# Squares summed along rows by ScalarE, and the down projection's weights in the common buffers

## The chip, the cores and the metric

The kernel runs on one core of a Trainium2 chip. A core has TensorE (matrix products), VectorE, ScalarE and GpSimd (work on elements), SyncE (here it only issues transfers), a memory SBUF of 128 partitions, and accumulators in PSUM, the only place that TensorE writes to. The metric is the time of one execution on the device in microseconds (us), as the median of several.

## The reference

One decoder layer for 256 tokens of width 2048, all in float32. `h @ w` are the products; the sizes of the weights set the work.

```python
h = rmsnorm(x, norm_mix)
q, k, v, u = split(h @ w_in)                     # 2048 -> 4 x 1024
o_attn = differential causal attention(q, k, v)  # 4 heads, each normalized
o_pool = trailing means of u over 2/4/8/16 positions, minus u; then a product per group
x = x + concat(o_attn, o_pool) @ w_o             # 2048 -> 2048
hx, m = rmsnorm(x, norm_xattn), rmsnorm(mem, norm_mem)   # mem: 256 tokens of width 2048
x = x + cross attention of hx into m (wq, wkv, wo: 2048 -> 2048, 4096, 2048)
hf = rmsnorm(x, norm_ffn)
x = x + (silu(hf @ w_gate) * (hf @ w_up)) @ w_down       # 2048 -> 5632 -> 2048
return rmsnorm(x, norm_final)

def rmsnorm(x, g):   # mean over the features of each token
    return x * rsqrt(mean(x * x, axis=-1) + 1e-6) * g
```

## The kernel before

**Split operands.** TensorE is fed in a float32 form that rounds. So each operand is split: `split` (L126) lets ScalarE write the rounded part `hi` (L129, or L132 with a gain) and VectorE the rest, `lo = src - hi` (L130, L133). A product is then hi x hi + hi x lo + lo x hi: three matmuls (`mm3`, L217 to L219), or, where activations stand with hi and lo side by side in 512 columns, one of 512 and one of 256 columns (L163, L164).

**Weights.** `weights` (L139) brings 1 MB of a weight by SyncE's queue into one of three buffers `raw`, and splits it in two halves of 128x1024 into `whi` and `wlo`, also three buffers each. All products up to gate and up take their weights so. `gemm_tok` (L191, matmuls L209 to L211) makes values by tokens, `gemm_feat` (matmuls L163, L164) by features.

**Order.** A scheduler places the instructions on each engine; an engine works through its own in that order and waits where an input or a buffer isn't free. `between` holds generators, which `tick` advances once per half tile of weights: pieces of other work are written between the halves in this way.

**Norms.** The gain is multiplied in when activations are split; the factor 1/rms, one for each token, is applied after the product. It is needed with tokens on partitions (`col`) and along a row (`row`). Activations stand with features on partitions, so a token's squares are spread over 128 partitions and 16 tiles. For x (`norm_x`, L323) and the memory (`load_mem`, L515), `add_squares` (L267) lets ScalarE square 1024 columns (L270) and GpSimd add them up (L272, L275). After the output projection and the cross-attention, `residual` (L277) adds each finished tile to x, splits it, lets ScalarE square it (L286) and GpSimd add it to a total (L288). `rms` (L248) sums a total over partitions by four small matmuls against ones (L254). `along` transposes `col` into a row.

**Bands.** For the pooling, GpSimd makes eight banded matrices by selects (L355 to L359) and adds two pieces for each (L361).

**Down projection** (`prep`, L714, and the loop behind it). 44 feature tiles of the activations make 22 pairs; the output has two blocks `b` of 1024 columns. A pair with its 1 MB of weights is a product of 2x2 blocks: eight products, 24 matmuls of 512 columns, for a plain pair; seven, 21 matmuls, for the pairs in `FAST` (even numbers 0 to 12), which need sums of weight blocks (VectorE, L731 to L734) and of activations, and whose shared products are accumulated apart (`shared`) and added up at the end (`sums`). The pools `dn_r` (two raw buffers, one for sums), `dn_u` (four split buffers of 128x1024) and `dn_a` (two of 128x1536) are made when the pools of the gate's stage, `hid` and `wts` among them, are closed (`up.close()`, L699).

## Time and profile before

| what | value |
|---|---|
| median of 3 runs | 1438.62 us (1438.57 to 1440.9) |
| profiled execution, its time | 1442.4 us |
| profiled execution, its span | 1440.7 us |
| TensorE busy (matmul) | 1409.7 us, 98% |
| VectorE busy | 970.5 us, 67% |
| ScalarE busy | 731.7 us, 51% |
| GpSimd busy | 82.5 us, 6% |
| DMA engines' mean share | 52% |

The span is cut by the profile into stretches; in each one reads how long each engine was busy, the clock that TensorE was granted (1.00 is 2.4 GHz, 0.50 is 1.2 GHz), and what the DMA engines moved. A timeline gives each instruction with its start and, in brackets, how long its engine was idle before it and what ended that.

### The profile page before, as it was taken

The page shows a single profiled execution, that of the slowest core. Times are in us where ns is not written, and L with a number is a line of the kernel's source. Part 1 is how long each engine was busy: PE and PEld are TensorE (multiplying, and loading weights), DVE is VectorE, ACT ScalarE, POOL GpSimd, SP SyncE. Part 2 cuts the span into 40 slices and gives each one's busy share as a digit, 9 for nine tenths or more (in the row PEclk, how much of TensorE's full clock was granted, in tenths as well). Part 3 has the DMA queues.
Part 4 walks back from the last instruction along what each step waited for, and adds up shares of the span by engine and source line. Part 5 has one row for each costly group of instructions (what it writes and reads, how often), then busy time and mean ns, then how long its engine had stood idle before and what let it go on. Part 6 is the DMA issues. An engine that isn't in the chain of part 4 may idle for free.

```text
span 1440.7 us, 19291 instructions
## 1 busy us (share of the span) xinstructions
PE 1409.7 (98%) x7634; PEld 1213.7 (84%) x7634; DVE 970.5 (67%) x1298; ACT 731.7 (51%) x1058; POOL 82.5 (6%) x103
## 2 busy tenths in 40 slices
PE   7999999899999999999999999999999998999996
PEld 5888888788888888888888888888888886888885
DVE  7566868875556655567666666666666668858963
ACT  6455657554444444455554444544444445535543
POOL 6400002210000000011100000000000000000000
PEclk9999999999999999999999999999999999999998
DMA  6554536455554554465655555555555536556752
GB/s 247 193 182 164 182 131 234 163 198 180 180 201 147 175 176 151 150 210 197 203 200 181 199 180 201 179 202 179 201 178 202 178 145 231 206 196 202 249 205 112
DMA packets 42570, 269.72 MB, mean 187 GB/s; under 512 B 4848, under 2 KB 5872, under 8 KB 12784
## 3 DMA queue, kind: packets, MB, share of 16 engines
q1 hardware_dynamic: 40032, 262.16, 52.0%
q10 hardware_dynamic: 2448, 6.34, 1.3%
q8 instruction: 59, 0.97, 0.3%
q14 instruction: 31, 0.25, 0.0%
HBM read 264.29 MB, written 4.19 MB: 186 GB/s over the span
## 4 chain that ended last, share of the span: by engine, by line
PE 94%; DVE 3%; ACT 1%; DMA 1%; issue 1%; SPq 0%; ACTq 0%; DVEq 0%
PE acc L163 42%; PE acc L164 21%; PE acc L218 4%; PE acc L219 4%; PE acc L217 4%; PE acc L209 4%; PE acc L210 4%; PE acc L211 4%; PE ms L218 2%; PE ms L219 2%; PE ms L217 2%; DMA raw<-in_w_vu 1%; DVE hid L133 1%; DVE wlo L130 1%; DVE act L133 1%
## 5 line engine op out<-in xcount | busy, mean ns | idle before, releaser
L130 DVE TENSOR_TENSOR wlo<-raw,whi 128x1024 fp32r<-128x1024 f32 (+1 forms) x404 | 496.9, 1231 | 330.5 <-ACT whi L129 327.3
L163 PE MATMUL acc<-hid,whi 128*128 128x512 f32 x1920 | 669.5, 394 | 0.0
L129 ACT CAST whi<-raw 128x1024 fp32r<-128x1024 f32 (+1 forms) x404 | 420.4, 1041 | 459.0 <-PE acc L163 241.6
L164 PE MATMUL acc<-hid,wlo 128*128 128x256 f32 x1920 | 533.6, 278 | 0.0
L163 PEld LDWEIGHTS acc<-hid,whi 128*128 128x128 f32 x1920 | 360.1, 188 | 83.3
L164 PEld LDWEIGHTS acc<-hid,wlo 128*128 128x128 f32 x1920 | 361.0, 188 | 0.0
L163 PE MATMUL acc<-act,whi 128*128 128x512 f32 x768 | 274.0, 400 | 0.0
L164 PE MATMUL acc<-act,wlo 128*128 128x256 f32 x768 | 216.6, 282 | 4.0 <-DVE wlo L130 3.9
L163 PEld LDWEIGHTS acc<-act,whi 128*128 128x128 f32 x768 | 145.0, 189 | 34.6
L164 PEld LDWEIGHTS acc<-act,wlo 128*128 128x128 f32 x768 | 145.9, 190 | 5.0 <-DVE wlo L130 4.9
L130 DVE TENSOR_TENSOR ul<-raw,uh 128x1024 fp32r<-128x1024 f32 x60 | 72.7, 1222 | 39.4 <-ACT uh L129 39.3
L217 PE MATMUL acc<-uh,aC 128*128 128x512 f32 x240 | 93.4, 389 | 0.0
L218 PE MATMUL acc<-ul,aC 128*128 128x512 f32 x240 | 93.4, 389 | 0.0
L219 PE MATMUL acc<-uh,aC 128*128 128x512 f32 x240 | 93.4, 389 | 0.0
L129 ACT CAST uh<-raw 128x1024 fp32r<-128x1024 f32 x60 | 62.6, 1052 | 59.6 <-PE acc L219 54.0
L210 PE MATMUL acc<-wlo,hid 128*128 128x512 f32 x128 | 51.1, 399 | 6.9 <-DVE wlo L130 6.8
L288 POOL TENSOR_TENSOR row<-row,t 128x256 f32<-128x256 f32 x30 | 27.0, 899 | 460.4 <-ACT t L286 460.4
L217 PEld LDWEIGHTS acc<-uh,aC 128*128 128x128 f32 x240 | 45.1, 188 | 9.4
L219 PEld LDWEIGHTS acc<-uh,aC 128*128 128x128 f32 x240 | 45.1, 188 | 9.4
L218 PEld LDWEIGHTS acc<-ul,aC 128*128 128x128 f32 x240 | 45.1, 188 | 9.2
L209 PE MATMUL acc<-whi,hid 128*128 128x512 f32 x128 | 50.7, 400 | 0.9 <-ACT whi L129 0.9
L211 PE MATMUL acc<-whi,hid 128*128 128x512 f32 x128 | 50.6, 395 | 0.0
(201 smaller groups left out, 1454.5 us busy)
## 6 DMA issues: line engine op xcount, KB each, us to landing
raw<-in_w_gu SPq DMA_DIRECT2D x88, 1024.0 KB, 4.8
raw<-in_w_dn SPq DMA_DIRECT2D x44, 1024.0 KB, 4.8
raw<-in_w_qk SPq DMA_DIRECT2D x16, 1024.0 KB, 4.8
raw<-in_w_qx SPq DMA_DIRECT2D x16, 1024.0 KB, 4.8
raw<-in_w_kx SPq DMA_DIRECT2D x16, 1024.0 KB, 4.8
raw<-in_w_vx SPq DMA_DIRECT2D x16, 1024.0 KB, 4.8
raw<-in_w_vu SPq DMA_DIRECT2D x12, 1024.0 KB, 4.8
raw<-in_w_o SPq DMA_DIRECT2D x12, 1024.0 KB, 4.9
```

Of the source, the lines that this page charges most:

```text
L129: nc.scalar.copy(out=hi, in_=src)
L130: nc.vector.tensor_tensor(out=lo, in0=src, in1=hi.bitcast(F32), op=ALU.subtract)
L133: nc.vector.scalar_tensor_tensor(out=lo, in0=src, scalar=g, in1=hi.bitcast(F32), op0=ALU.mult, op1=ALU.subtract)
L163: nc.tensor.matmul(ps, whi[:, w], x, start=(k == 0), stop=False)
L164: nc.tensor.matmul(ps[:, :S], wlo[:, w], x[:, 0], start=False, stop=(k == nk - 1))
L209: nc.tensor.matmul(ps[t], xh, whi[:, w], start=(k == 0), stop=False)
L210: nc.tensor.matmul(ps[t], xh, wlo[:, w], start=False, stop=False)
L211: nc.tensor.matmul(ps[t], xl, whi[:, w], start=False, stop=(k == KT - 1))
L217: nc.tensor.matmul(ps, l[0], r[0], start=start, stop=False)
L218: nc.tensor.matmul(ps, l[0], r[1], start=False, stop=False)
L219: nc.tensor.matmul(ps, l[1], r[0], start=False, stop=stop)
L288: nc.gpsimd.tensor_tensor(out=tot, in0=tot, in1=sq, op=ALU.add)
```

## The change

It has three parts, and a few constants that follow from them (`PAD` keeps the places of pools in memory).

**Squares by rows.** `add_squares` and `norm_x` go, and `rms` stays for one norm alone. `row_squares` loads x, or the memory, once more with tokens on partitions (new inputs `x_rows`, `mem_rows`; two transfers of 1 MB each on SyncE's queue), and ScalarE squares 1024 columns at a time and sums them along the row in the same instruction (`accum_out`). VectorE adds the two halves. For the norm before gate and up, the row copies of x that `to_rows` makes anyway are squared in this way, and the factor is made after the first two tiles of gate and up instead of after the first. `residual` keeps its squares for the cross-attention's norm only, and VectorE adds them instead of GpSimd. The band matrices' additions also go to VectorE.

**Weights of the down projection.** The pool `wts` is now opened first and lives to the end. `prep` takes `raw`, `whi` and `wlo` from it (three buffers each); sums of weight blocks are written over raw blocks or into a small buffer `sum`. A pair with seven products hands out its parts in four pieces of two, two, two and one block instead of three of three, two and two.

**Which pairs.** `FAST` becomes the nine even numbers 2 to 18; pairs 0 and 1 are plain.

```diff
-FAST = tuple(range(0, 14, 2))
+FAST = tuple(range(2, 20, 2))
...
+    wts = ctx.enter_context(tc.tile_pool(name="wts", bufs=3, side="right"))
     hid = up.enter_context(tc.tile_pool(name="hid", bufs=4, side="right"))
-    wts = up.enter_context(tc.tile_pool(name="wts", bufs=3, side="right"))
...
+    def row_squares(src, r):
+        ss = const.tile([P, 2, 2], F32, name=name("ss"))
+        for t in range(2):
+            raw = slot(F32)
+            nc.sync.dma_start(out=raw, in_=src[:, t])
+            for _ in range(2):
+                yield
+            for h in range(2):
+                part = raw[:, h * 1024:(h + 1) * 1024]
+                nc.scalar.activation(out=part, in_=part, func=AF.Square, accum_out=ss[:, t, h:h + 1])
+                yield
+        rc = const.tile([P, 2], F32, name=name("rc"))
+        nc.vector.tensor_reduce(out=rc, in_=ss, axis=AX.X, op=ALU.add)
+        r["col"] = rsqrt(rc, rc, D)
+        yield
+        r["row"] = t_row()
+        nc.vector.tensor_copy(out=r["row"], in_=along(rc))
...
-        sq = tot if f == 0 else t1()
-        nc.scalar.activation(out=sq, in_=x, func=AF.Square)
-        if 0 < f and (into is not None or f < KT - 1):
-            nc.gpsimd.tensor_tensor(out=tot, in0=tot, in1=sq, op=ALU.add)
+        if tot is not None:
+            sq = tot if f == 0 else t1()
+            nc.scalar.activation(out=sq, in_=x, func=AF.Square)
+            if f:
+                nc.vector.tensor_tensor(out=tot, in0=tot, in1=sq, op=ALU.add)
...
-    between.append(norm_x())
+    between.append(row_squares(a["x_rows"], r_x))
...
-            nc.gpsimd.tensor_tensor(out=band[:, kt, g], in0=b, in1=dgn, op=ALU.add)
+            nc.vector.tensor_tensor(out=band[:, kt, g], in0=b, in1=dgn, op=ALU.add)
...
-            add_squares(tot, c, raw)
...
+        yield from row_squares(a["mem_rows"], r_m)
...
+            nc.scalar.activation(out=t2(), in_=tp, func=AF.Square, accum_out=ss_x[:, t, q:q + 1])
...
-    nc.vector.tensor_copy(out=rb_f, in_=along(rms(tot2)))
     ps_u = gemm_feat(hf, a["w_gu"][1])
     finish()
+    rc_f = const.tile([P, 2], F32, name="rc_f")
+    nc.vector.tensor_reduce(out=rc_f, in_=ss_x, axis=AX.X, op=ALU.add)
+    rb_f = const.tile([P, S], F32, name="rb_f")
+    nc.vector.tensor_copy(out=rb_f, in_=along(rsqrt(rc_f, rc_f, D)))
...
-        raw = dn_r.tile([P, 4, 512], F32, tag="raw", name=name("raw"))
+        raw = wts.tile([P, 4, 512], F32, tag="raw", name=name("raw"))
...
-        s = dn_r.tile([P, 4, 512], F32, tag="sum", bufs=1, name=name("sum"))
-        nc.vector.tensor_tensor(out=s[:, 0:2], in0=b12[:, None].to_broadcast([P, 2, 512]), in1=raw[:, 0:2], op=ALU.subtract)
-        yield halves(raw[:, 0:3], 3, dn_a, "a")
-        nc.vector.tensor_tensor(out=s[:, 2], in0=b22, in1=s[:, 0], op=ALU.subtract)
-        nc.vector.tensor_tensor(out=s[:, 3], in0=b21, in1=s[:, 2], op=ALU.subtract)
-        yield halves(s[:, 0:2], 2, dn_u, "u")
-        yield halves(s[:, 2:4], 2, dn_u, "u")
+        yield parts(raw[:, 0:2])
+        s = dec.tile([P, 2, 512], F32, tag="sum", bufs=2, name=name("sum"))
+        less(s, b12[:, None].to_broadcast([P, 2, 512]), raw[:, 0:2])
+        yield parts(s)
+        less(b12, b22, s[:, 0])
+        yield parts(raw[:, 2:4])
+        less(b22, b21, b12)
+        yield parts(raw[:, 1:2], 1)
...
-            if p == 14 and FAST:
+            if p in FAST[-1:]:
                 between.append(sums(b, [shared[0], None, shared[1], shared[2], shared[3]]))
```

How the instructions stand then is shown at three places. GpSimd's queue at the start, before (`act` is the total of squares and then the bands, `t` the selects):

```order
L357 AFFINE_SELECT t_65_518<-t_65_518 128x256
L272 TENSOR_TENSOR act_322<-act_322 128x1024 x3
L275 TENSOR_TENSOR act_322<-act_322 128x512
L275 TENSOR_TENSOR act_322<-act_322 128x256
L361 TENSOR_TENSOR act_493<-t_60_499,t_61_500 128x256
L361 TENSOR_TENSOR act_493<-t_62_506,t_63_507 128x256
L359 AFFINE_SELECT t_66_519<-t_64_513 128x256
```

and the same queue, now:

```order
L353 AFFINE_SELECT t_65_512<-t_65_512 128x256
L355 AFFINE_SELECT t_66_513<-t_64_507 128x256
L350 MEMSET t_67_519 128x256
L355 AFFINE_SELECT t_68_520<-t_64_507 128x256
L351 AFFINE_SELECT t_67_519<-t_67_519 128x256
L344 MEMSET t_69_526 128x256
L353 AFFINE_SELECT t_67_519<-t_67_519 128x256
```

Five additions of squares and the bands' additions are gone from it; the selects follow each other, as buffers come free.

VectorE's queue at the entry of the down projection, before (`raw` to `ul` are the first pair's weights, `t1f` and `aC` the last activations):

```order
L661 TENSOR_TENSOR t1f_10712<-acc_10669,t1f_10712 128x256
L691 TENSOR_TENSOR t1f_10712<-t1f_10712,rb_f 128x256
L661 TENSOR_TENSOR t1f_10760<-acc_10717,t1f_10760 128x256
L694 TENSOR_TENSOR t1f_10760<-t1f_10760,rb_f 128x256
L696 TENSOR_TENSOR t1f_10668<-t1f_10712,t1f_10760 128x256
L130 TENSOR_TENSOR aC_10568<-t1f_10668,aC_10568 128x256
L731 TENSOR_TENSOR sum_10793<-raw_10791 128x1024
L733 TENSOR_TENSOR sum_10793<-raw_10791,sum_10793 128x512
L734 TENSOR_TENSOR sum_10793<-raw_10791,sum_10793 128x512
L130 TENSOR_TENSOR al_10796<-raw_10791,ah_10795 128x1536
L130 TENSOR_TENSOR ul_10811<-sum_10793,uh_10810 128x1024
```

and now (the first row is the first half of pair 0):

```order
L130 TENSOR_TENSOR wlo_10739<-raw_10736,whi_10738 128x1024
L653 TENSOR_TENSOR t1f_10667<-acc_10624,t1f_10667 128x256
L683 TENSOR_TENSOR t1f_10667<-t1f_10667,rb_f 128x256
L130 TENSOR_TENSOR wlo_10755<-raw_10736,whi_10754 128x1024
L716 TENSOR_TENSOR sum_10816<-raw_10804 128x1024
L130 TENSOR_TENSOR wlo_10773<-raw_10770,whi_10772 128x1024
L653 TENSOR_TENSOR t1f_10715<-acc_10672,t1f_10715 128x256
L716 TENSOR_TENSOR raw_10804<-raw_10804,sum_10816 128x512
L686 TENSOR_TENSOR t1f_10715<-t1f_10715,rb_f 128x256
L688 TENSOR_TENSOR t1f_10623<-t1f_10667,t1f_10715 128x256
L130 TENSOR_TENSOR aC_10523<-t1f_10623,aC_10523 128x256
L130 TENSOR_TENSOR wlo_10789<-raw_10770,whi_10788 128x1024
```

The first pair's splits have moved from behind the last activations to ahead of them, between the evictions of the last tiles of gate and up.

VectorE's queue a little further on in the down projection, at the second pair with seven products, before:

```order
L130 TENSOR_TENSOR ul_10821<-sum_10793,uh_10820 128x1024
L130 TENSOR_TENSOR ul_10833<-raw_10830,uh_10832 128x1024
L130 TENSOR_TENSOR ul_10849<-raw_10830,uh_10848 128x1024
L731 TENSOR_TENSOR sum_10866<-raw_10864 128x1024
L733 TENSOR_TENSOR sum_10866<-raw_10864,sum_10866 128x512
L130 TENSOR_TENSOR al_10869<-raw_10864,ah_10868 128x1536
L734 TENSOR_TENSOR sum_10866<-raw_10864,sum_10866 128x512
L130 TENSOR_TENSOR ul_10884<-sum_10866,uh_10883 128x1024
L130 TENSOR_TENSOR ul_10894<-sum_10866,uh_10893 128x1024
```

and now, at the first such pair (pair 2; `sum_10893` belongs to pair 4):

```order
L130 TENSOR_TENSOR wlo_10807<-raw_10804,whi_10806 128x1024
L716 TENSOR_TENSOR raw_10804<-raw_10804 128x512
L130 TENSOR_TENSOR wlo_10819<-sum_10816,whi_10818 128x1024
L716 TENSOR_TENSOR sum_10893<-raw_10881 128x1024
L130 TENSOR_TENSOR wlo_10830<-raw_10804,whi_10829 128x1024
L130 TENSOR_TENSOR wlo_10841<-raw_10804,whi_10840 128x512
L130 TENSOR_TENSOR wlo_10850<-raw_10847,whi_10849 128x1024
L716 TENSOR_TENSOR raw_10881<-raw_10881,sum_10893 128x512
L130 TENSOR_TENSOR wlo_10866<-raw_10847,whi_10865 128x1024
L130 TENSOR_TENSOR wlo_10884<-raw_10881,whi_10883 128x1024
L716 TENSOR_TENSOR raw_10881<-raw_10881 128x512
```

Before, a pair's first sum stood with its own pair's splits. Now it stands ahead of the last two splits of the seven-product pair before it; in later pairs it stands behind those and ahead of the plain pair's.

## Rows read from the trace of the kernel before

**Rows 1.** Page's span and TensorE's share (busy us, share, instructions)

```profile
span 1440.7 us, 19291 instructions
...
PE 1409.7 (98%) x7634; PEld 1213.7 (84%) x7634; DVE 970.5 (67%) x1298; ACT 731.7 (51%) x1058; POOL 82.5 (6%) x103
```

**Rows 2.** Waits of TensorE: us in total, times, longest us

```profile
PE acc L210 <- DVE wlo L130: 6.8, 5, 3.9
PE ms L217 <- ACT ah L129: 4.5, 1, 4.5
PE acc L164 <- DVE wlo L130: 3.9, 2, 2.6
```

**Rows 3.** Three stretches: length, busy us by engine, granted clock, DMA share, GB/s

```profile
14.00:36.00 22.00, 15.41 (x57) 11.32 (x56) 19.87 (x17) 12.34 (x19) 16.39 (x12) 0.92 0.68 256
...
240.00:269.00 29.00, 25.03 (x131) 20.95 (x130) 28.82 (x34) 17.63 (x29) 15.02 (x10) 0.94 0.48 171
1189.00:1200.50 11.50, 6.59 (x22) 4.65 (x21) 9.14 (x11) 6.04 (x7) 0.00 (x0) 0.70 0.64 222
```

**Rows 4.** Timeline of TensorE at the start: start us, us, operation, [idle before]

```profile
17.15 0.39 PE L209 MATMUL acc<-whi,hid 128*128 128x512 f32 x1
18.87 0.50 PE L210 MATMUL acc<-wlo,hid 128*128 128x512 f32 x1 [1.33 <-DVE wlo L130]
...
27.55 0.39 PE L209 MATMUL acc<-whi,hid 128*128 128x512 f32 x1
31.81 0.52 PE L210 MATMUL acc<-wlo,hid 128*128 128x512 f32 x1 [3.87 <-DVE wlo L130]
...
34.26 0.63 PE L210 MATMUL acc<-wlo,hid 128*128 128x512 f32 x1
34.69 0.63 PE L211 MATMUL acc<-whi,hid 128*128 128x512 f32 x1
```

**Rows 5.** Same time on VectorE, GpSimd and ScalarE

```profile
14.46 0.69 DVE L130 TENSOR_TENSOR wlo<-raw,whi 128x512 fp32r<-128x512 f32 x1
...
16.35 2.47 DVE L130 TENSOR_TENSOR wlo<-raw,whi 128x512 fp32r<-128x512 f32 x1 [0.80 <-ACT whi L129]
...
15.88 2.39 POOL L272 TENSOR_TENSOR act<-act 128x1024 f32<-128x1024 f32 x1 [8.94 <-ACT act L270]
...
16.91 1.71 ACT L132 ACTIVATE hid<-x_sb,sm 128x256 fp32r<-128x256 f32 x4 [0.60 <-DMA x_sb<-in_xT]
18.52 1.03 ACT L129 CAST whi<-raw 128x1024 fp32r<-128x1024 f32 x1
```

**Rows 6.** Output projection: VectorE and GpSimd

```profile
236.62 0.48 DVE L133 SCALAR_TENSOR_TENSOR act<-act,sm,act 128x256 fp32r<-128x256 f32 x1
...
241.50 2.62 DVE L133 SCALAR_TENSOR_TENSOR hid<-x_sb,sm,hid 128x256 fp32r<-128x256 f32 x1
...
240.99 2.85 POOL L272 TENSOR_TENSOR act<-act 128x1024 f32<-128x1024 f32 x1 [1.16 <-ACT act L270]
```

**Rows 7.** Stretches: the DMA queue backed up; down projection's first block

```profile
20.00:22.00 2.00, 1.16 (x6) 0.65 (x5) 2.00 (x4) 2.00 (x4) 1.40 (x1) 1.00 1.08 416
...
1200.50:1311.00 110.50, 110.50 (x489) 91.55 (x488) 84.19 (x80) 54.70 (x51) 0.00 (x0) 1.00 0.59 205
```

**Rows 8.** VectorE while GpSimd makes selects

```profile
48.23 1.75 DVE L130 TENSOR_TENSOR wlo<-raw,whi 128x1024 fp32r<-128x1024 f32 x1 [1.28 <-ACT whi L129]
```

**Rows 9.** Chain of waits: start us, us, piece (a norm's sums; the pace)

```profile
706.20 0.34 PE ms L254 x4
...
1202.69 0.23 PE acc L218
```

**Rows 10.** Groups by line: count, busy us, mean ns, idle before

```profile
L130 DVE TENSOR_TENSOR ul<-raw,uh 128x1024 fp32r<-128x1024 f32 x60 | 72.7, 1222 | 39.4 <-ACT uh L129 39.3
...
L734 DVE TENSOR_TENSOR sum<-raw,sum 128x512 f32<-128x512 f32 x14 | 9.6, 684 | 0.0
```

**Rows 11.** Page's DMA issues: count, KB, us to landing

```profile
raw<-in_w_dn SPq DMA_DIRECT2D x44, 1024.0 KB, 4.8
```

78 lines of the change are left out of this document (25 added, 53 removed).

## The prediction

> **What bounds the kernel now.** I read the page first: TensorE is busy for 1409.7 us of a span of 1440.7 us [rows 1]. A matmul's end is modelled, so that share says only that every microsecond won must be one in which TensorE stands still or runs slowly, or a matmul left out. Next I read whom TensorE waits for [rows 2]. All that counts is three waits on a split of a weight (ScalarE casts the high part, VectorE subtracts for the low one): 6.8 us and 3.9 us for VectorE's low parts, 4.5 us for ScalarE's cast. Third, I cut the span into stretches [rows 3]: these waits lie in 14 to 36 us (the first projection), 240 to 269 us (the output projection, while the memory's activations are split beside it) and 1189 to 1200.5 us (the entry of the down projection). There the granted clock falls below 1.00 and TensorE is idle; elsewhere it keeps its pace.
>
> What a stretch loses is its idle time, what slow matmuls cost, and some 0.27 us at each stop, since the last matmul's busy time reaches 0.16 us past its turn and the first after a stop takes 0.11 us longer. The start: 22.00 - 15.41 = 6.6 us idle [rows 3], in four stops, of which the first and last stand in [rows 4]. After the last, nine matmuls come 0.43 us apart [rows 4] instead of 0.23, at the level of 1.2 GHz after an idle 3.87 us: 9 x 0.20 = 1.8 us. With 4 x 0.27 that is 9.5 us. The output projection: 29.00 - 25.03 = 4.0 us idle; a clock of 0.94 over 29 us means about 3.5 us at half speed, so 1.7 us lost; three stops give 0.6: 6.2 us, an estimate. The entry: 11.50 - 6.59 = 4.9 us idle, nine slow matmuls 1.8 us, two stops 0.6: 7.3 us.
>
> **Why VectorE is late there.** At the start a subtraction of 128x512 takes 2.47 us where the seven of its size before it take 0.62 to 0.80 (the last of them 0.69) [rows 5]; GpSimd's addition of squares began just ahead, at 15.88 us, and ran 2.39 us. At 241.5 us it is the same: 2.62 us for a split that took 0.48 us at 236.6, under a GpSimd addition of 2.85 us [rows 6]. Two engines off the chain, summing squares for norms, stop the chain.
>
> The Trainium skill (SBUF — State Buffer, Who interferes with whom) says that a VectorE instruction with two SBUF inputs contends with a GpSimd instruction that reads SBUF, and the later one blocks until the other is done. The rows agree: 16.35 + 2.47 ends 0.55 us after GpSimd's 18.27.
>
> **The change part by part.**
>
> *Squares of x.* The four squares on ScalarE and GpSimd's five additions leave the start; with them goes the cause of the stops. What is late next is the DMA queue: the cast of the third weight tile cannot start before 18.52 us [rows 5], since ScalarE first has four splits of x that landed at 16.9. Then the cast 1.03, VectorE 1.2: TensorE goes on at about 20.8 us, not at 21.6, and stood still for about 2.0 us from 18.5 (17.15 [rows 4] and six matmuls). The rest of that projection then has its splits in time, VectorE needing about 4.1 us per tile (2 x 1.22 and four splits of x at 0.4) against 24 x 0.227 = 5.5 us of TensorE. So 9.5 - 2.0 - 0.2 = **7.3 us** are won.
>
> Instead x is loaded a second time by rows, 2 x 1 MB on SP's queue, one ahead of the second, one ahead of the fourth weight tile of the next projection. The weights queue behind them. The DMA engines moved 416 GB/s while backed up [rows 7], so 1 MB is 2.5 us; each tile is wanted 5.5 us after the one before and has over 3 us in hand: nothing. The squares (four, each like a cast of its size, 1.03 us [rows 5], and a read of the sum) and the reduction lie beside the second projection's matmuls; then the root, and v's evictions, which release the accumulators that the third projection needs. In the order they stand ahead of the last tile's splits, 5 us before TensorE wants them: nothing. But the eight additions for the bands go from GpSimd to VectorE, between v's evictions and the second tile's split of the third projection. Eight x 0.42 us on VectorE (estimated below), with GpSimd's selects making their inputs. While such selects ran, VectorE's split took up to 1.75 us instead of 1.22 [rows 8]. By my count of that queue the split is done about when it is wanted. Bounds: 0, and 1.5 us (three instructions lengthened by 0.5 us); I take **0.4 us lost**, near the lower end because the splits after it have slack again. By the skill's rule taken strictly, each of the eight additions could stand behind a whole select; the sum would then be 8 x 0.4 = 3.2 us of VectorE, and the loss about 2 us rather than 0.4.
>
> *Squares of the memory, and of the sums after the output projection.* The memory's squares move to the next projection (4 on ScalarE, 2 x 1 MB on SP), where a tile of weights takes TensorE 5.6 us and ScalarE about 3: hidden. In 240 to 269 us, VectorE loses the long waits (three of about 2.1 us, and shorter ones under GpSimd's smaller additions) and takes GpSimd's additions of 256 columns, one per feature tile of 5.6 us, about 0.42 us each (an estimate: 512 columns take 0.69 [rows 10]). It was busy for all of this stretch before; without about 8 us of waiting and with 2 us of additions it is at some 75%. So the stops go: **6.0 us won**; if the additions ahead of a split still cost one stop, 3.
>
> *Three norms without a sum over partitions.* `rms` on TensorE goes for x, the memory and the feed-forward norm; each is 0.34 us [rows 9]: **1.0 us**. The third norm's transposes move behind the first gate and up tiles. Their chain (square, reduce, load of the root's table, root, reciprocal) ends some 8 us after the last x tile, and eleven matmuls stand ahead of the transposes; ScalarE has 1 us or more free per cast there: nothing. Its squares, now eight of 512 columns in the row copies for sixteen of 256, stand ahead of the stores to DRAM, which nobody waits for until the down projection.
>
> *Entry of the down projection.* Before, its buffers were new pools over memory of the gate's tiles, and its first pair needed a sum and splits of three parts; now raw and splits come from the same pool as all weights, and the first pair is plain. Transfer, cast and subtraction of pair 0 stand ahead of the last evictions, and TensorE goes from the last up tile straight into pair 0. What is late next is the last up tile's eviction (behind a 1.05 us cast, then 0.37 and 0.42 us), which frees the fourth accumulator; it is wanted after twelve matmuls, 2.7 us. All 7.3 us of the entry go, or 0.2 of them stay: **7.2 us won**.
>
> *Nine pairs with seven products.* Two more pairs of 22, in two blocks, each with three matmuls fewer: 12 x 0.23 us [rows 9] = **2.7 us**, if VectorE keeps up. For two pairs it has six instructions of 1.22 us and three of 0.69 [rows 10]: 9.4 us at most, against (24 + 21) x 0.227 = 10.2 us of TensorE. It fits; VectorE was at 76% before [rows 7].
>
> *Three buffers instead of up to six.* A tile's cast waits until TensorE has left the tile three before. Cast 1.05, subtraction 1.22, and 0.2 for the signals: 2.5 us; for the first tile of a plain pair TensorE has in that time only the last two tiles of the seven, 6 + 3 matmuls, 2.05 us, and one or two on the high part. So TensorE may wait 0 to 0.3 us at each of 18 places; I take 0.05, since the high part's matmuls go ahead: **0.9 us lost**, bounds 0 and 5.4. And in the second block VectorE's queue has the sum for pair 4, which waits for its transfer of 4.8 us [rows 11], ahead of a split of pair 2; the evictions of the first block make this the tightest place. 0 to 2 us; **0.5 us lost**.
>
> The sum: 7.3 + 6.0 + 1.0 + 7.2 + 2.7 = 24.2, less 0.4 + 0.9 + 0.5 = 1.8: **22.4 us won**. The profiled execution took 1442.4 us, of which 1.7 lie around the span; it would become 1420.0. The median of the other runs lies 3.8 us lower, at 1438.6, and the same gain gives **1416.2 us**.
>
> **The rivals.** (1) *Three buffers are too few*: the handover costs its upper bound, 5.4 us, and the second block's start 2: 1422 us. For it: the margin is a few tenths. Against it: the gate's tiles, on the same three buffers, wait nowhere. (2) *The start and the output projection keep part of their stops*, because the loads by rows delay weights (2 x 2.5 us at most) or VectorE, now with the additions, is still late (3 us): 1421 us. Against it: slack of 3 us and a load of 75%. (3) *Slower than before*: VectorE's queue stands at each sum of the next seven-product pair until its weights land, and all splits queue behind. There are 18 such sums; it decides from 1.25 us at each, since 18 x 1.25 = 22.5 us eats the gain; at 2 us, 1452 us. For it: the buffer is freed by the last split of the pair three before, and VectorE has then only about 5 us of work ahead of the sum, little more than the 4.8 us of the transfer. Against it: VectorE is held back by TensorE's pace, which adds some 2 us. (4) *It does not do what it says*: pair 0's weights cannot be split early, since the memory or the queue holds them, and the entry stays: 1423 us.
>
> **How the numbers follow.** The forecast 0.72 (1411 to 1420: upper gains, no new waits, and up to 3 us for the pace of matmuls with moved buffers), (1) 0.10, (2) 0.09, (4) 0.03, (3) 0.05, nothing measurable 0.01. A range from 1411 to 1424 leaves out (3) and parts of the tails. Faster by over 0.2% (2.9 us, about what a measurement of this kernel can tell from no change): 0.94; within: 0.01; slower: 0.05.
>
> **What would show it.** No wait of TensorE on a split over 1 us after 25 us; granted clock 1.00 in 26 to 36, 232 to 262 and around the entry; VectorE's splits at the start at 0.5 and 1.2 us throughout; the third projection's first tiles and the pairs of the down projection without stops. Wrong if TensorE waits in each pair, or if VectorE's sums wait for weights.

## The result and the profile after

The changed kernel took 1425.09 us (median of 4 executions, 1421.82 to 1426.48), the kernel before in the same comparison 1439.76 us (4, 1438.57 to 1441.32): a ratio of 0.9894 with a 95% interval of 0.9873 to 0.9916. That is 14.7 us won; 22.4 had been forecast, with a range that ended at 1424. A second comparison (the first experiment below) gave 1423.05 us against 1440.61, a ratio of 0.9877 (0.9858 to 0.9896), 17.6 us. So the sign and most of the mechanism were right, and 5 to 8 us of the gain are missing.

The page of the changed kernel, which answers to [rows 1]:

```profile
span 1422.6 us, 19276 instructions
...
PE 1404.4 (99%) x7610; PEld 1208.7 (85%) x7610; DVE 967.5 (68%) x1361; ACT 742.3 (52%) x1083; POOL 23.6 (2%) x55
```

TensorE has 24 instructions fewer, GpSimd is down from 82.5 to 23.6 us. Whom TensorE waited for (us in total, times, longest), all that is left of its waits on a split [rows 2]:

```profile
PE acc L210 <- DVE wlo L130: 1.5, 3, 0.8
PE acc L209 <- ACT whi L129: 1.5, 2, 1.1
```

The waits of 3.9, 2.6 and 4.5 us are gone. The same stretches as in [rows 3], moved by what was won ahead of them, and at the end the stretch of the down projection that answers to the second of [rows 7] (length, busy us of TensorE, its weight loads, VectorE, ScalarE, GpSimd, then the granted clock, DMA share, GB/s):

```profile
14.00:36.00 22.00, 20.35 (x88) 15.89 (x87) 13.63 (x20) 14.54 (x22) 0.00 (x0) 1.00 1.01 411
232.00:262.00 30.00, 30.00 (x174) 26.26 (x173) 27.00 (x49) 19.70 (x34) 0.00 (x0) 1.00 0.67 240
1173.00:1184.50 11.50, 11.50 (x59) 9.59 (x58) 8.98 (x13) 5.49 (x9) 0.00 (x0) 1.00 0.74 268
1184.50:1295.00 110.50, 110.43 (x481) 89.19 (x480) 92.65 (x98) 60.31 (x66) 0.00 (x0) 1.00 0.59 201
```

The granted clock is 1.00 in all of them, and of the first three TensorE stands still only in that at the start, for 1.65 us instead of 6.59. But look at the last: in 110.5 us there were 489 matmuls before [rows 7], and there are 481 now, with hardly any idle time shown. At the pace of [rows 9] eight matmuls are 1.8 us.

To see where the time went, the start of the same matmul is looked up in both traces, at the seams of the stages. "Again" is the second profiled execution of the changed kernel.

| stage, from one seam to the next | before, us | after | again | won | won again | forecast |
|---|---|---|---|---|---|---|
| start to the third projection's first matmul | 61.45 | 53.99 | 53.89 | 7.5 | 7.6 | 7.6 |
| third projection (to 83.31, 77.14, 77.05) | 21.86 | 23.15 | 23.16 | -1.3 | -1.3 | -0.4 |
| from there to gate and up's last matmul | 1106.72 | 1100.24 | 1099.54 | 6.5 | 7.2 | 6.7 |
| from that to the down projection's last | 237.13 | 231.34 | 231.08 | 5.8 | 6.1 | 8.5 |
| to the end of the span | 13.54 | 13.88 | 13.82 | -0.3 | -0.3 | 0 |
| span | 1440.7 | 1422.6 | 1421.5 | 18.1 | 19.2 | 22.4 |

(Of the three norms at 0.3 us, the first is in the forecast's first row, the two others are in the third.) Two stages fall short: the third projection by 0.9 us, the down projection by 2.4 to 2.7.

**The third projection.** TensorE, then VectorE, then GpSimd:

```profile
66.35 0.50 PE L210 MATMUL acc<-wlo,hid 128*128 128x512 f32 x1 [0.79 <-DVE wlo L130]
```

```profile
63.49 0.60 DVE L357 TENSOR_TENSOR act<-t,t 128x256 fp32r<-128x256 f32 x1 [1.26 <-POOL t L353]
64.74 0.43 DVE L357 TENSOR_TENSOR act<-t,t 128x256 fp32r<-128x256 f32 x1 [0.64 <-POOL t L353]
65.08 3.49 DVE L130 TENSOR_TENSOR wlo<-raw,whi 128x1024 fp32r<-128x1024 f32 x3
```

```profile
63.78 0.57 POOL L355 TENSOR_SCALAR_AFFINE_SELECT t<-t 128x256 f32<-128x256 f32 x1
64.31 0.40 POOL L353 TENSOR_SCALAR_AFFINE_SELECT t<-t 128x256 f32<-128x256 f32 x1
```

VectorE isn't busy ahead of the late subtraction: it stands still for 1.26 and 0.64 us, since the band additions (L357) stand in its queue and wait for GpSimd's selects. The eight additions themselves take 0.41 to 0.60 us, near the 0.42 of the estimate.

**The down projection.** The view of waits names what ScalarE's casts wait for there, a buffer that TensorE still reads, and in the second line what holds up TensorE's weight loads (PEld), 20 times.

```profile
ACT whi L129 <- PE ms L219: 14.6, 24, 0.7
...
PEld acc L218 <- DVE wlo L130: 6.4, 20, 0.6
```

One of the 20 places, on ScalarE, VectorE and TensorE:

```profile
1201.88 1.06 ACT L129 CAST whi<-raw 128x1024 fp32r<-128x1024 f32 x1 [0.69 <-PE ms L219]
```

```profile
1201.99 1.22 DVE L716 TENSOR_TENSOR sum<-raw 128x1024 f32<-128x1024 f32 x1
1203.12 1.22 DVE L130 TENSOR_TENSOR wlo<-raw,whi 128x1024 fp32r<-128x1024 f32 x1
```

```profile
1203.72 0.84 PE L217 MATMUL acc<-whi,aC 128*128 128x512 f32 x3
1204.40 0.50 PE L218 MATMUL acc<-wlo,aC 128*128 128x512 f32 x1
1204.74 0.40 PE L219 MATMUL acc<-whi,aC 128*128 128x512 f32 x1
```

This is the first tile of a plain pair. Three matmuls on the high part have run ahead; the fourth needs the low part, which VectorE ends at 1204.34. The matmul starts at 1204.40 and the next 0.34 us later instead of 0.23: the 0.11 us after a stop that the prediction had read from [rows 4], here after a stop too short to show as idle time. Over the 1001 intervals of the down projection the excess over 0.2267 us is 4.3 us (again: 4.0), some 0.2 us for each of the 20 places on the mean, from 0.1 us where only the restart is paid to 0.6. Two causes offer themselves in these rows: the buffer (the cast stood 0.69 us waiting for it), and the sum (1.22 us) in VectorE's queue ahead of the subtraction, whose cast had ended at 1202.94.

### The profile page after: what moved, and what is told of

The parts are those of the page before. It is cut to its first block, busy times and chain, and to the rows that moved or that the text cites. A ratio compares the mean times of both kernels' runs of the same rounds, so it can differ in the third digit from the quotient of the medians.

```text
span 1422.6 us, 19276 instructions
## 1 busy us (share of the span) xinstructions
PE 1404.4 (99%) x7610; PEld 1208.7 (85%) x7610; DVE 967.5 (68%) x1361; ACT 742.3 (52%) x1083; POOL 23.6 (2%) x55
## 4 chain that ended last, share of the span: by engine, by line
PE 93%; DVE 2%; DMA 2%; ACT 1%; POOL 1%; issue 0%; SPq 0%; DVEq 0%
PE acc L163 44%; PE acc L164 22%; PE acc L218 4%; PE acc L219 4%; PE acc L210 4%; PE acc L211 4%; PE acc L209 3%; PE acc L217 3%; PE ms L218 2%; PE ms L219 2%; PE ms L217 2%; DVE wlo L130 1%; DMA raw<-in_w_dn 1%; DMA raw<-in_w_vu 1%; ACT whi L129 0%
## 5 line engine op out<-in xcount | busy, mean ns | idle before, releaser
L130 DVE TENSOR_TENSOR wlo<-raw,whi 128x1024 fp32r<-128x1024 f32 (+1 forms) x510 | 606.5, 1196 | 360.7 <-ACT whi L129 357.6
L129 ACT CAST whi<-raw 128x1024 fp32r<-128x1024 f32 (+1 forms) x510 | 523.2, 1029 | 527.0 <-PE acc L163 250.6
L163 PE MATMUL acc<-hid,whi 128*128 128x512 f32 x1920 | 670.7, 393 | 0.0
L164 PE MATMUL acc<-hid,wlo 128*128 128x256 f32 x1920 | 538.1, 280 | 0.0
L163 PEld LDWEIGHTS acc<-hid,whi 128*128 128x128 f32 x1920 | 359.6, 187 | 80.8
L164 PEld LDWEIGHTS acc<-hid,wlo 128*128 128x128 f32 x1920 | 362.9, 189 | 0.0
L163 PE MATMUL acc<-act,whi 128*128 128x512 f32 x768 | 271.9, 398 | 0.0
L164 PE MATMUL acc<-act,wlo 128*128 128x256 f32 x768 | 215.5, 281 | 0.0
L163 PEld LDWEIGHTS acc<-act,whi 128*128 128x128 f32 x768 | 144.2, 188 | 34.0
L164 PEld LDWEIGHTS acc<-act,wlo 128*128 128x128 f32 x768 | 145.1, 189 | 0.2
L218 PE MATMUL acc<-wlo,aC 128*128 128x512 f32 x208 | 83.1, 399 | 0.4
L219 PE MATMUL acc<-whi,aC 128*128 128x512 f32 x208 | 81.2, 390 | 0.0
L217 PE MATMUL acc<-whi,aC 128*128 128x512 f32 x208 | 75.2, 390 | 0.0
L218 PEld LDWEIGHTS acc<-wlo,aC 128*128 128x128 f32 x208 | 39.0, 188 | 13.2 <-DVE wlo L130 5.7
L209 PE MATMUL acc<-whi,act 128*128 128x512 f32 x128 | 50.0, 390 | 0.0
L210 PE MATMUL acc<-wlo,act 128*128 128x512 f32 x128 | 49.9, 390 | 0.0
L211 PE MATMUL acc<-whi,act 128*128 128x512 f32 x128 | 49.8, 389 | 0.0
L129 ACT CAST act<-t 128x256 fp32r<-128x256 f32 x48 | 19.5, 406 | 54.9 <-DVE t L225 54.9
L217 PEld LDWEIGHTS acc<-whi,aC 128*128 128x128 f32 x208 | 39.0, 188 | 8.8 <-DVE t1f L653 0.2
```

Source lines behind the costliest of these rows:

```text
L129: nc.scalar.copy(out=hi, in_=src)
L130: nc.vector.tensor_tensor(out=lo, in0=src, in1=hi.bitcast(F32), op=ALU.subtract)
L163: nc.tensor.matmul(ps, whi[:, w], x, start=(k == 0), stop=False)
L164: nc.tensor.matmul(ps[:, :S], wlo[:, w], x[:, 0], start=False, stop=(k == nk - 1))
L209: nc.tensor.matmul(ps[t], xh, whi[:, w], start=(k == 0), stop=False)
L210: nc.tensor.matmul(ps[t], xh, wlo[:, w], start=False, stop=False)
```

## The experiments

### The same kernel again

> The changed kernel, unaltered, profiled and timed once more. Theory: its first trace shows a gain of 18.1 us over the trace of before, while the medians showed 14.7 us, because each single execution lies anywhere in a spread of 4 to 5 us; then a second trace has the same stops of TensorE in the same places (one in the third projection, some twenty short ones in the down projection), and the medians of more executions differ by 16 to 18.5 us (ratio 0.987 to 0.989). Rival: the profiled execution of before was slowed by being profiled, as the prediction took it, and that of after was not; then the medians stay 14 to 15.5 us apart (ratio 0.989 to 0.9905), and the missing part isn't in the traces.

Measured: 1423.05 us (4 executions, 1420.92 to 1424.83), before 1440.61 (7, 1438.71 to 1444.3). The second trace has the same stops (20 weight loads held up in the down projection, 6.3 us; 1.3 us lost in the third projection). The profiled execution of before, 1442.4 us, lies high among the executions of that kernel, which reach from 1434.15 to 1444.3 us over all comparisons, with medians of 1439.76 to 1440.61; that of after, 1424.28, lies in the middle of its own. Over the changed kernel and the eleven experiments with several executions, the profiled execution lies between 2.1 us under and 2.1 us over the median of its comparison, 0.1 over on the mean. So a profile costs no 3.8 us: the prediction took a draw for an offset. From a median of some 1440.2 the forecast gain would have ended at 1417.8, not at 1416.2.

### Down projection: the order on VectorE, the buffers, both

First the sum alone is queued later (`issue_after` orders two instructions on one engine):

```diff
+        with tc.issue_after(lo_split[-2].ins):   # the plain pair's second subtraction
+            less(s, b12[:, None].to_broadcast([P, 2, 512]), raw[:, 0:2])
-        less(s, b12[:, None].to_broadcast([P, 2, 512]), raw[:, 0:2])
```

> Only the order on VectorE in the down projection: each seven-product pair's first sum (128x1024, 1.22 us) is queued behind the low-part subtraction of that pair's first tile or of the plain pair ahead of it, where it now stands ahead of the plain pair's first subtraction. Theory A (VectorE's queue): TensorE's short stops at the plain pair's first tile come from the sum ahead of its subtraction; they go, and 3 to 4.3 us are won against the changed kernel (ratio to it about 0.9975). Theory B (three buffers): the stops come from the cast, which waits until TensorE has left the tile three before; then the stops stay, and the time changes by less than 1 us.

Measured: 1423.39 us (1423.08 to 1423.72), the changed kernel beside it 1423.05. There is no gain, as theory B has it. The same place as above, ScalarE, VectorE and TensorE:

```profile
1201.19 1.06 ACT L129 CAST whi<-raw 128x1024 fp32r<-128x1024 f32 x1 [0.69 <-PE ms L219]
```

```profile
1202.27 3.72 DVE L130 TENSOR_TENSOR wlo<-raw,whi 128x1024 fp32r<-128x1024 f32 x3 [0.85 <-ACT whi L129]
```

```profile
1203.56 0.50 PE L218 MATMUL acc<-wlo,aC 128*128 128x512 f32 x1
1203.89 0.39 PE L219 MATMUL acc<-whi,aC 128*128 128x512 f32 x1
```

VectorE now stands idle (0.85 us) until the cast is through and starts at once, and TensorE still stops: 18 weight loads held up, 5.7 us in all, and 3.9 us lost over the down projection. The chain of buffer, cast and subtraction is too long by itself.

Then a fourth pair of buffers alone:

```diff
+    ex = ctx.enter_context(tc.tile_pool(name="ex", bufs=1, side="right", reuse_waits="tile"))
...
+            pool = ex if len(made) % 4 == 0 else wts     # every fourth tile
-            hi = wts.tile([P, 1024], F32R, tag="whi", name=name("whi")).rearrange("p (s n) -> p s n", s=2)
+            hi = pool.tile([P, 1024], F32R, tag="whi", name=name("whi")).rearrange("p (s n) -> p s n", s=2)
...
```

> A fourth pair of buffers for high and low parts in the down projection; three stay for everything ahead of it. The order that the scheduler makes of VectorE's queue changes with it: a pair's first sum then stands ahead of the last, 512 wide subtraction of the pair before. Theory B (three buffers are too few): the short stops go, 3 to 4.3 us are won against the changed kernel. Theory A (VectorE's queue): the sum, now earlier still, stands in the queue before its weights have landed (4.8 us after the buffer is free), so VectorE waits there and TensorE's stops get longer: slower by up to 18 x 1 us, or no gain at all.

Measured: 1423.47 us (1421.53 to 1425.54); again no gain. But the trace is another one (two of the waits, then VectorE and TensorE at one place):

```profile
DVE sum L720 <- DMA raw<-in_w_dn: 13.7, 11, 2.9
...
PEld acc L218 <- DVE wlo L130: 4.0, 7, 1.2
```

```profile
1203.70 1.23 DVE L720 TENSOR_TENSOR sum<-raw 128x1024 f32<-128x1024 f32 x1 [2.58 <-DMA raw<-in_w_dn]
```

```profile
1207.32 0.50 PE L218 MATMUL acc<-wlo,aC 128*128 128x512 f32 x1 [0.77 <-DVE wlo L130]
```

Most of the 20 short stops are gone. In their place VectorE waits for transfers at the sums, 11 times, and where that wait is long TensorE stops for up to 0.77 us; 3.2 us are still lost over the down projection. This is the prediction's third rival, in small. Both theories were half right, so both edits together:

> The changed kernel with both edits of the down projection at once: a fourth pair of buffers for high and low parts, and each seven-product pair's first sum queued on VectorE behind the subtractions of the plain pair ahead. Theory: the short stops need both, since three buffers hold the cast of the plain pair's first tile back (the stops stayed when only the sum went later) and, with four, the sum stood in the queue before its weights had landed (waits of 2.0 to 2.6 us for the transfer). Now the down projection runs at 0.227 us a matmul throughout, and loses under 1 us over its 1002 matmuls, where the changed kernel lost 4.1 and 4.3: about 3.5 us faster than it, 1419 to 1421 us. Rival: a third thing (the reuse of the raw tiles, ScalarE's queue) is late next, and 2 us or more stay lost.

Measured: 1419.76 us (4, 1419.13 to 1420.91), a ratio to before of 0.9861 (0.9844 to 0.9878). That interval overlaps with those of the changed kernel, so the stage itself has to decide. The whole down projection of this kernel, and the same of the changed one:

```profile
1178.00:1405.50 227.50, 227.50 (x1004) 187.83 (x1002) 194.25 (x207) 125.91 (x137) 0.00 (x0) 1.00 0.58 204
```

```profile
1177.50:1409.00 231.50, 231.12 (x1004) 186.15 (x1002) 194.06 (x207) 123.98 (x137) 0.00 (x0) 1.00 0.58 200
```

The same 1004 matmuls in 4 us less; the excess over 0.2267 us a matmul is 0.3 us. So the missing part of the down projection is shown: it was the handover, and it needed both a buffer and the order.

### Seven pairs instead of nine

```diff
-FAST = tuple(range(2, 20, 2))
+FAST = tuple(range(2, 16, 2))
```

> The changed kernel with seven pairs of seven products (plain pair first, pairs 2, 4, ... 14) instead of nine. Theory: two pairs in each of the two blocks need three matmuls of 0.227 us more, 2.7 us, but four of the twenty short stops, of 0.2 us each, go: 1.9 us slower than the changed kernel. Rival: plain pairs, with four wide splits where the seven-product pair has seven in two pairs, let VectorE catch up, so that more of the stops go and the two come out the same within 0.5 us.

Measured: 1426.46 us (1424.36 to 1427.48), 2.4 us above the mean of the changed kernel's two medians; but the ratio, 0.9904 (0.9886 to 0.9922), has an interval that overlaps with those of the changed kernel. In the trace 16 weight loads are held up instead of 20, and the down projection takes 232.9 us, 1.6 to 1.8 us more than in the changed kernel's two traces. Twelve matmuls are 2.7 us, and four stops take a third of that back.

### The two parts alone

The sums of squares alone, in the kernel before:

```diff
-    between.append(norm_x())
+    between.append(row_squares(a["x_rows"], r_x))
...
-            nc.gpsimd.tensor_tensor(out=band[:, kt, g], in0=b, in1=dgn, op=ALU.add)
+            nc.vector.tensor_tensor(out=band[:, kt, g], in0=b, in1=dgn, op=ALU.add)
...
-        residual(f, ps, tot1, col(C_XAT + f), hx[-1])
+        residual(f, ps, col(C_XAT + f), hx[-1], tot1)
```

And the down projection alone, in the kernel before:

```diff
-FAST = tuple(range(0, 14, 2))
+FAST = tuple(range(2, 20, 2))
...
-        raw = dn_r.tile([P, 4, 512], F32, tag="raw", name=name("raw"))
+        raw = wts.tile([P, 4, 512], F32, tag="raw", name=name("raw"))
```

> The kernel before with the sums of squares alone changed (rows on ScalarE, the bands' and the output projection's additions on VectorE, no sum over partitions on TensorE); the down projection as before, with its own pools and seven pairs. By the traces of the changed kernel, TensorE reaches the end of the last gate and up tile 12.7 to 13.4 us earlier than before. Theory: the two parts don't meet, so this part alone wins 12 to 13.5 us (ratio 0.991 to 0.992) and the entry of the down projection keeps its stops of 4.5 us and after. Rival: the earlier stages leave more time to the loads for the down projection, so the entry gets shorter too, and this part alone wins over 15 us.

> The kernel before with the down projection alone changed (buffers of all weights, plain pair first, nine pairs with seven products); the squares as before. Theory: 5 to 6 us won (7.3 of the entry, 2.7 of twelve matmuls, less 4.3 of some twenty short stops and 0.3 in the tail): ratio 0.9955 to 0.9965, with the stops of the start and of the output projection as before. Rival: the short stops come with the other part (its loads or ScalarE's squares); then this part alone wins 9 to 10 us, and the down projection's matmuls stay at 0.227 us throughout.

Measured: 1431.26 us (6 executions) and 1434.72 us (6) against 1440.03 (11): ratios 0.9940 (0.9924 to 0.9955) and 0.9962 (0.9948 to 0.9976), 8.8 and 5.3 us. The second is as expected. The first is short of the 12 to 13.5 us, which were taken from traces against the high draw of before; in its own trace TensorE is 11.5 us ahead at the end of gate and up, and the start is worse by 1.1 us for reasons told at the end. The entry keeps its stop without the second part:

```profile
PE ms L217 <- ACT ah L129: 4.3, 1, 4.3
```

The sum of the two, 14.1 us, agrees with the 14.7 and 17.6 us of the whole within the intervals; that the parts meet somewhere by a microsecond or two isn't excluded.

The trace of the second part alone also shows how far the trace of before is a draw. Up to the third projection its instructions are those of before, in the same order on each engine; yet it gets there at 59.83 us, 1.6 us earlier, and the longest stop at the start, 3.87 us in [rows 4], is shorter:

```profile
30.49 0.79 PE L210 MATMUL acc<-wlo,hid 128*128 128x512 f32 x1 [2.92 <-DVE wlo L130]
```

At the end of gate and up, all of it unchanged work but for where pools lie in memory, it is 2.4 us ahead of the trace of before; the execution behind that trace, 1442.4 us, is 2.2 us above the later medians. So the gains of the table above, all taken against that one trace, may be too high by about as much.

The trace of the second part alone has, early in the second block, the place at which the prediction set 0.5 us (0 to 2). The run with the bands (below) has it too, and there the rows of VectorE and TensorE read:

```profile
1302.36 1.23 DVE L718 TENSOR_TENSOR sum<-raw 128x1024 f32<-128x1024 f32 x1 [1.36 <-DMA raw<-in_w_dn]
```

```profile
1305.50 0.50 PE L218 MATMUL acc<-wlo,aS 128*128 128x512 f32 x1 [1.23 <-DVE wlo L130]
```

It cost 1.5 us in these two executions, and nothing in the two of the changed kernel: the wait exists, but not in each trace, and whether the kernel or the execution decides isn't shown. The two plain pairs behind it cost 0.5 us each in all four, where most others cost 0.1.

### GpSimd's additions on VectorE, and GpSimd's work where nobody waits

In the kernel before, only the engine of the additions of squares is changed:

```diff
-            nc.gpsimd.tensor_tensor(out=tot[:, :1024], in0=tot[:, :1024], in1=part, op=ALU.add)
+            nc.vector.tensor_tensor(out=tot[:, :1024], in0=tot[:, :1024], in1=part, op=ALU.add)
...
-            nc.gpsimd.tensor_tensor(out=tot, in0=tot, in1=sq, op=ALU.add)
+            nc.vector.tensor_tensor(out=tot, in0=tot, in1=sq, op=ALU.add)
```

> The kernel before with one change: GpSimd's additions of squares (at the start, for the memory, and after each output tile) are put on VectorE; the squares themselves, their places and the sums on TensorE stay. Theory: what stops TensorE at the start and in the output projection is GpSimd's additions, beside which VectorE's splits take 2.5 us where they take 0.5 to 1.2; most of the 9.5 us and 6.2 us lost there go, though VectorE now has three additions of 1.2 us, two smaller ones and 16 of 0.4 us more: 10 to 13 us won (ratio 0.991 to 0.993), and no split of 512 columns above 0.8 us. Rival: it is the work itself, or ScalarE's squares ahead of its casts, on whichever engine; then the stops stay and at most 4 us are won.

Measured: 1433.12 us (6) against 1440.03, ratio 0.9954 (0.9937 to 0.997), 6.9 us; between theory and rival. Its two stretches:

```profile
14.00:36.00 22.00, 18.99 (x74) 14.70 (x74) 21.64 (x27) 13.62 (x21) 14.43 (x22) 0.92 0.74 274
232.00:262.00 30.00, 30.00 (x172) 26.02 (x171) 29.09 (x52) 24.01 (x40) 0.00 (x0) 1.00 0.66 240
```

In the output projection TensorE has no stop any more; by the starts of its matmuls 6.0 us are won there, the forecast's very term. At the start only 3.1 us come (1.5 against the draw of 59.83 us), and the granted clock is 0.92 again: VectorE is busy for 21.64 of 22 us, its additions of 1024 columns (1.41 us each) stand ahead of splits, and GpSimd still adds and selects for the bands beside it (14.43 us). So at the start it wasn't enough that the work changed engines. In the changed kernel it is gone: the sum that ScalarE makes along a row leaves VectorE one small reduction.

The price itself, in the changed kernel, with idle work for GpSimd in gate and up:

```diff
+        if p in (5, 7, 9):
+            nc.gpsimd.tensor_tensor(out=p0[:, :S], in0=y, in1=p1[:, :S], op=ALU.add)
+            for _ in range(6):
+                nc.gpsimd.tensor_tensor(out=p2, in0=p0, in1=p1, op=ALU.add)
+        if p in (13, 15, 17):
...
+                nc.gpsimd.affine_select(out=p2, in_=p0, pattern=[[1, 512]], compare_op=ALU.is_ge, fill=0.0,
+                                        base=0, channel_multiplier=-1)
```

> The changed kernel with extra work on GpSimd in the gate and up projections, where TensorE waited for nothing and VectorE has slack: behind each of three pairs' products six additions (two inputs, 128x512), and behind each of three later ones six selects (one input, 128x512). Nothing uses their results. Theory (two-input instructions of GpSimd and VectorE shut each other out): VectorE's subtractions of 1024 columns, 1.2 us elsewhere, take 2 to 3 us beside additions; beside selects they take 1.2 to 1.8 us. Rival: GpSimd slows VectorE by its share of the memory alone; then additions lengthen a subtraction no more than selects do, to 1.8 us at most.

Measured: 1432.87 us in one execution, which was profiled. In gate and up, 129 of VectorE's subtractions of 1024 columns with none of this work beside them take 1.22 us. 18 that run beside selects, for most or for a third of their time, take 1.24 to 1.60, the median 1.41; 21 that begin while additions run take 1.61 to 2.32, the median 2.31. Three more begin just ahead of an addition: they keep their 1.22 us, and the addition, of 256 columns, takes 1.59 us instead of 0.74. GpSimd's row of additions, then VectorE's beside it:

```profile
816.90 11.75 POOL L665 TENSOR_TENSOR probe<-probe,probe 128x512 f32<-128x512 f32 x6
```

```profile
819.26 2.31 DVE L130 TENSOR_TENSOR wlo<-raw,whi 128x1024 fp32r<-128x1024 f32 x1
821.49 0.41 DVE L653 TENSOR_TENSOR t1f<-acc,t1f 128x256 f32<-128x256 f32 x1
821.94 1.07 DVE L701 TENSOR_TENSOR t1f<-t1f,rb_f 128x256 f32<-128x256 f32 x1
822.93 4.55 DVE L130 TENSOR_TENSOR wlo<-raw,whi 128x1024 fp32r<-128x1024 f32 x2
```

And the same beside selects:

```profile
998.76 5.93 POOL L670 TENSOR_SCALAR_AFFINE_SELECT probe<-probe 128x512 f32<-128x512 f32 x6
```

```profile
1001.34 1.40 DVE L130 TENSOR_TENSOR wlo<-raw,whi 128x1024 fp32r<-128x1024 f32 x1 [0.82 <-ACT whi L129]
1004.17 1.60 DVE L130 TENSOR_TENSOR wlo<-raw,whi 128x1024 fp32r<-128x1024 f32 x1 [0.63 <-ACT whi L129]
```

So selects lengthen a subtraction by up to 0.4 us, additions by 1.1 at the median, which the rival excludes. Of the rows beside the additions, two are alike but for one input: L653 reads an accumulator in PSUM and a tile, and takes 0.41 us as always; L701 reads two tiles in SBUF, and takes 1.07 instead of 0.42. That is what the Trainium skill (SBUF — State Buffer, Who interferes with whom) says: a VectorE instruction with two inputs in SBUF contends with a GpSimd instruction that reads SBUF. The section makes no difference between GpSimd's instructions with one input and with two; here the measured prices differ, up to 0.4 us against 1.1.

### The bands

The additions for the bands back on GpSimd:

```diff
-            nc.vector.tensor_tensor(out=band[:, kt, g], in0=b, in1=dgn, op=ALU.add)
+            nc.gpsimd.tensor_tensor(out=band[:, kt, g], in0=b, in1=dgn, op=ALU.add)
```

> The eight additions for the bands back on GpSimd, all else as in the changed kernel. Theory: TensorE's stop of 0.95 us in the third projection (and the one of 0.3 us) comes from these additions standing in VectorE's queue, each waiting for GpSimd's selects, ahead of the split; it goes, and 1.2 us are won (TensorE reaches the end of the third projection 1.2 us earlier). Rival: the stop comes from GpSimd slowing VectorE's own instructions in this stretch, whichever engine adds; then the stop stays, or grows by 0.5 us with GpSimd's additions, which read two inputs as well.

Measured: 1426.14 us (1423.87 to 1427.54), 3.1 above the changed kernel beside it; the 1.2 us of the theory were not won. The stop in the third projection is gone (25.00 us busy in the 25 us from 53 to 78, 24.21 in the changed kernel), but the third projection begins at 55.38 us, where the four traces of the changed kernel and its variants so far have 53.2 to 54.0: GpSimd, which needn't wait for VectorE now, goes on with its selects and additions at the start, for 19.54 us of the 20 from 5 to 25, and there they block. Its row at one place, VectorE's split beside it (0.48 us in the changed kernel), and TensorE's longest stop:

```profile
16.76 1.16 POOL L357 TENSOR_TENSOR act<-t,t 128x256 fp32r<-128x256 f32 x1
```

```profile
17.25 0.96 DVE L133 SCALAR_TENSOR_TENSOR hid<-x_sb,sm,hid 128x256 fp32r<-128x256 f32 x1
```

```profile
22.68 0.50 PE L210 MATMUL acc<-wlo,hid 128*128 128x512 f32 x1 [1.72 <-DVE wlo L130]
```

So the move of the additions to VectorE, which the prediction booked as a loss alone, had bought 1.4 us or more of the start, by this one trace. The two amounts cancel: at the end of the third projection it stands at 77.25 us, the changed kernel at 77.14 and 77.05. So the 3.1 us of the medians aren't the bands'; in this trace they are lost between there and the end, and why isn't shown. The early start and a third projection without a stop are both to be had if the selects run in between:

```diff
+            r.setdefault("raw", []).append(raw.rearrange("p (i t) -> p i t", i=8))
...
-            b, dgn = t1(), t1()
+            i = 4 * (g % 2) + 2 * kt     # in the tiles that the rows of x have left free
+            b, dgn = r_x["raw"][g // 2][:, i], r_x["raw"][g // 2][:, i + 1]
```

> The changed kernel, with GpSimd's selects for the bands put into the tiles that the rows of x leave free, so that GpSimd doesn't wait for a tile until VectorE has added, and works during the second projection; the eight additions stay on VectorE. Theory: the stop of 0.95 us and the one of 0.3 in the third projection come from VectorE's queue waiting for selects; they go, and the end of the third projection comes 1.2 us earlier (TensorE is 7.4 to 7.5 us ahead of before there, instead of 6.2 to 6.9). Rival: the selects, now beside the second projection's splits, slow these as they did in the trace of before (1.75 us instead of 1.22), and the stops only change place: no gain.

Measured: 1424.63 us (5) against 1440.03, ratio 0.9891 (0.9875 to 0.9907): no gain that the time shows against the changed kernel, whose two ratios lie about it. The trace agrees with the theory: no stop in the third projection, TensorE 8.1 us ahead of before at its beginning and still 8.1 at its end, and the selects at 31 to 49 us lengthen no wait of TensorE. It lost 1.5 us later, at the second block (above), and the price of the plain pairs as before.

All three edits together:

> All three edits that removed a stop: four buffers, the sum queued later, and the selects for the bands during the second projection. Theory: the gains add, 3.5 us in the down projection and 1.2 us in the third projection: 1418 to 1420 us, ratio to before 0.985 to 0.986. Rival: the stages between take it back, since the weights' pace in the output projection and the projections behind it is 0.353 us per pair of matmuls in some executions and 0.347 in others, whatever stands ahead; then the median comes out as with the two edits alone, within 1 us.

Measured: 1418.87 us (5, 1418.07 to 1420.43), ratio to before 0.9851 (0.9834 to 0.9868); the fastest of all, 0.9 us below the two edits alone, which its spread does not tell from nothing. Of TensorE's waits on a split only those at the start are left, 2.5 us.

## Why the prediction was right or wrong

**Right.** The start: 7.3 us forecast, 7.1 and 7.2 measured without the norm (7.5 and 7.6 with it). What was to be late next was the third tile's cast at 18.5 us, and it is: it comes at 18.97, and TensorE goes on at 20.05 for two matmuls on the high part and at 21.31 for good, where the sum had "about 20.8". The mechanism holds; that the size agrees to 0.2 us is luck in part, since forecast and measurement share the one trace of before. Against the other execution of the same start (59.83 us) it is 5.5. The output projection: 6.0 us, measured 6.0 with the additions moved alone. Its cause, GpSimd's two-input additions beside VectorE's two-input splits, holds by the run in gate and up. One row was misread on the way: beside the split of 1.75 us in [rows 8] ran not only selects but, from 48.16 us for 0.73, an addition for the bands. The entry: the last matmul of gate and up and the first of the down projection stand 0.12 us apart.

```profile
1177.38 0.28 PE L164 MATMUL acc<-hid,wlo 128*128 128x256 f32 x1
1177.50 0.39 PE L217 MATMUL acc<-whi,aC 128*128 128x512 f32 x1
```

Twelve fewer matmuls: 2.7 us, and with seven pairs the stage is 1.6 to 1.8 us longer. Rival 2 did not come, since the output projection has no stop and the start only those of the sum; nor did rivals 3 and 4; the sums do wait for weights in places, as rival 3 says, but twice (1.2 us), not 18 times.

**Wrong: the handover, 0.9 us, measured 4.0 and 4.3.** The step was "TensorE may wait 0 to 0.3 us at each of 18 places; I take 0.05, since the high part's matmuls go ahead". Many of the waits are as small as that, but a stop has no small price: even where it is too short to show as idle time, the first matmul after it takes 0.11 us more, a number that the prediction had. A place costs nothing, or 0.1 us and more, here 0.2 on the mean; 0.05 would have needed three places in four without a stop, and nothing said so, since the places are much alike. The chain also left out the sum that stands ahead of the subtraction, though the order of VectorE's queue showed it; with a fourth buffer that is what remains. The bound of 5.4 us held, and rival 1 (1422 us) was the better forecast, with luck: it adds 2 us at the second block's start, where nothing was lost in these two traces that isn't in the 4.0 and 4.3. By the prediction's own sign, TensorE waiting in the pairs, it was wrong here.

**Wrong: the third projection, 0.4 us, measured 1.3.** The additions were priced as instructions that GpSimd slows down. Each was also a new wait, of VectorE for GpSimd, in a queue with a split behind it. The bounds (0 to 1.5) held. The 2 us that the prediction set beside it, for additions that stand behind whole selects, did not come either: the additions took 0.41 to 0.60 us. In turn the same move gave the start more room, which wasn't seen either.

**Wrong: the level.** 3.8 us between the profiled execution and the median were carried over as an offset. They were the spread: 1.6 us of the miss in time come from a first median of 1438.6 where later ones are at 1439.8 to 1440.6. And what the three stretches lose was read from a slow draw, 2.4 us of it not there in another execution of the same stages, so the gain was forecast too high by about as much.

**Not decided.** By medians 14.7 and 17.6 us were won, by traces 18.1 and 19.2, or 15.7 and 16.8 without the 2.4 us of the draw. Of the 4.8 to 7.7 us that are missing, 3.3 to 3.6 are thus the handover and the third projection (net of the 0.5 set for the second block), and some 2.4 the draw; the rest is within the spread of single executions.

## What to carry to other kernels

A split that hands tiles to TensorE needs one buffer more than its chain (buffer free, cast, subtraction, signals) fits into, and nothing in the queue ahead of its last step: here either edit alone gave nothing that the time showed, and both took 3.8 to 4.0 us off the stage. Price a possible stop of TensorE at its restart or at nought, never in between. Do not read what a stage loses from a single trace. When work moves from one engine to another, count two things besides its own time: whom the new owner now waits for, and what the old one, set free, will run into earlier.

## What the hardware showed unasked

**Two paces of the same matmuls.** A pair of matmuls of 512 and 256 columns (L163, L164) takes 0.347 us in some stretches and 0.353 in others, at a granted clock of 1.00, for tens or hundreds of microseconds on end; which of the two differs between executions of one program. The output projection and the projection behind it, in the changed kernel and in its second execution:

```profile
240.00:270.00 30.00, 30.00 (x175) 26.36 (x174) 26.27 (x45) 17.13 (x27) 0.00 (x0) 1.00 0.55 185
320.00:350.00 30.00, 30.00 (x173) 26.06 (x172) 17.73 (x25) 15.25 (x24) 0.00 (x0) 1.00 0.55 192
```

```profile
240.00:270.00 30.00, 30.00 (x172) 26.00 (x172) 25.92 (x44) 16.70 (x25) 0.00 (x0) 1.00 0.52 180
320.00:350.00 30.00, 30.00 (x176) 26.50 (x175) 18.29 (x25) 16.48 (x27) 0.00 (x0) 1.00 0.55 183
```

Here 175 matmuls, then 173; there 172, then 176. Gate and up keep the faster pace in every run but the one with GpSimd's idle work, which shows what a slip may cost:

```profile
700.00:816.00 116.00, 116.00 (x672) 102.21 (x671) 77.82 (x115) 59.64 (x85) 0.53 (x1) 1.00 0.55 192
1060.00:1176.00 116.00, 116.00 (x659) 100.50 (x658) 78.17 (x108) 55.77 (x81) 13.16 (x16) 1.00 0.53 183
```

From 837 us on, where VectorE was late, the pace is the slower one until the stage ends, through stretches in which nobody waits; 8.4 us went there, of which the three stops are 1.8 us. The two paces are part of the executions' spread. What sets the pace is open: no run here changes one thing that would tell.

**The same stops, another clock.** In the changed kernel TensorE stood still for 1.07 and 0.52 us at 18.6 and 20.4 us, and the granted clock stayed at 1.00. With the squares alone, the same instructions up to there, it stood still for 1.08 and 0.52 us at the same place, and the clock fell: 0.92 over 14 to 36 us, matmuls 0.43 us apart (the level of 1.2 GHz) from 21.5 to 24 us.

```profile
14.00:36.00 22.00, 20.27 (x80) 15.61 (x80) 13.44 (x18) 13.77 (x23) 0.00 (x0) 0.92 0.99 386
```

That cost 1.6 us over nine matmuls. With the bands' additions on GpSimd a stop of 1.72 us left the clock at 1.00. So whether a short stop cost more than itself was not a matter of its length alone.
